# A decoder block on one core: first stage and last sums issued in program order, the norm's scale vector spread by TensorE

## The chip, the cores and the metric

The kernel runs on one core of a Trainium2 chip (trn2). The metric is the device time of one execution in microseconds (us). Three executions of the kernel before took 2191.38, 2193.44 and 2195.94 us; the median, 2193.44 us, is its time here.

The core has five engines that each run their own instructions one after the other: TensorE (PE in the rows, with PEld for its weight loads), VectorE (DVE), ScalarE (ACT), GpSimd (POOL) and SyncE (SP), which here issues most of the DMAs. They wait for each other by semaphores.

## The reference, cut to what matters

One layer, 512 rows of 2048 values in float32:

```python
def rmsnorm(x, g):
    return x * lax.rsqrt(jnp.mean(x * x, axis=-1, keepdims=True) + EPS) * g

h = rmsnorm(x, g_mix_pre)
mix = hybrid_mixer(h, w_in, w_out, ...)      # four attention mixers on the columns of h @ w_in
x = x + rmsnorm(mix, g_mix_post)
h2 = rmsnorm(x, g_mlp_pre)
y = jnp.square(jax.nn.relu(h2 @ w_up)) @ w_down
x = x + rmsnorm(y, g_mlp_post)
```

Only the two ends matter here: the first norm with the few columns of `h @ w_in` that are wanted with rows on the partitions (values of two attention branches, gates and forget logits: 288 columns), and the last norm with its sum.

## The kernel before, in words

Every matrix product is made of three float32r products (high by high, high by low, low by high), so each operand is split: ScalarE casts the high part and VectorE subtracts it to get the low part (`split`, L90 to L92).

**First stage (L160 to L239).** The 512 rows are four tiles `t` of 128 rows. Per tile: a DMA loads `x` (3 buffers); ScalarE squares it with a running sum (L194); GpSimd makes the reciprocal root `r` (L86, L87); VectorE scales four chunks of 512 columns by `r` and by `gB` (L213), the vector `g_mix_pre` on all 128 partitions, loaded by a broadcast DMA of 1 MB (L183); TensorE transposes each chunk in four 128x128 pieces (L154) into one of three PSUM banks `mm`; `split` moves it to `acth` and `actl`. The value weights come in four chunks of 512 rows (L176, 2 buffers `raw`, four DMAs each) and are split to `wvh` and `wvl`. Then 48 matmuls per tile (16 row blocks, three products each; L218 to L220) add up 288 columns in one of two PSUM banks `pt`, and `split` (to `vA`), an exponential (`gates`) and an addition (`fy`) read that bank (L221 to L223). Two small matmuls on a table of the relative bias (L232) and their sums `row` (L233) belong to the stage as well. Behind it come the large projections, `mm<-acth,wh` at L311.

A scheduler at build time puts each engine's instructions in an order of its own, by its estimate of when their inputs are there; it may take matmuls of one tile between those of another, and pieces of later work (such as `wl<-raw,wh`, the split of the first projections' weights) between those of the stage. On the chip an engine then takes its instructions in that order.

**End (L1364 to L1375).** The second product of the MLP ends with a chain of 24 matmuls into bank `a`, 12 for row tile 2 and 12 for row tile 3. For each of the two tiles VectorE adds the bank to `ze` (L1371), ScalarE squares and sums it (L1241), VectorE adds the parts of the sum (L1255) and GpSimd takes the root, VectorE multiplies by `g_mlp_post` (L1246) and adds the scaled result to `x` (L1262, two halves `zn` and `ze`), and DMAs store it (L1264). The `zn` halves of both tiles are squared and scaled shortly before (`done`, L1248; scaled on GpSimd).

Of the kernel before, what the change touches and what calls it, by code (L numbers as in the profile page):

```python
# [10 lines left out]
F32 = mybir.dt.float32  # L11
# [27 lines left out]

@with_exitstack  # L40
def hybrid_block(ctx: ExitStack, tc: tile.TileContext, a, out):
    nc = tc.nc
# [117 lines left out]
    with tc.tile_pool(name="start", bufs=1, reuse_waits="tile") as st:  # L160
# [10 lines left out]
        def load_v(c):  # L171
            raw = wa.r.tile([128, 4, 512], F32, name="raw", tag="raw", bufs=wa.raw)
            ks_ = slice(4 * c, 4 * c + 4)
            o = 0
            for col, w in ((VSA, 128), (VWA, 128), (GA, 24), (FC, 8)):
                nc.sync.dma_start(raw[:, :, o:o + w], w_in_k[:, ks_, col:col + w])  # L176
                o += w
            split(wvh[:, ks_], wvl[:, ks_], raw[:, :, 0:VW])

        gB = st.tile([128, D], F32, name="gB")  # L180
        nc.scalar.dma_start(ident, a["c_ident"])
        load_x(0)
        nc.sync.dma_start(gB, bcast_rows(a["g_mix_pre"], 128, D))  # L183
        load_v(0)
        load_x(1)
        load_x(2)
        load_v(1)
        load_v(2)
        load_v(3)
        ss = st.tile([128, NT], F32, name="ss")  # L190
        junk = st.tile([128, D], mybir.dt.bfloat16, name="junk")
# [5 lines left out]
        rs = [mean_square(0)]  # L197
# [3 lines left out]
        foxb = st.tile([128, 8], F32, name="foxb")  # L201
        nc.scalar.dma_start(foxb, bcast_rows(a["fox_bias"], 128, 8))


        for t in range(NT):
            r = rs[t]
            if t + 1 < NT:
                if t == 0:
                    load_x(3)
                rs.append(mean_square(t + 1))  # L210
            for c in range(4):
                cs = slice(512 * c, 512 * (c + 1))
                nc.vector.scalar_tensor_tensor(xs[t][:, cs], xs[t][:, cs], r[:, 0:1], gB[:, cs],  # L213
                                               op0=OP.mult, op1=OP.mult)
                transpose_into(xs[t][:, cs], t, 4 * c)
            o = bank("pt")
            for k in range(KT):
                nc.tensor.matmul(o[:, 0:VW], acth[:, k, tb(t)], wvh[:, k], start=(k == 0), stop=False)  # L218
                nc.tensor.matmul(o[:, 0:VW], acth[:, k, tb(t)], wvl[:, k], start=False, stop=False)
                nc.tensor.matmul(o[:, 0:VW], actl[:, k, tb(t)], wvh[:, k], start=False, stop=(k == KT - 1))  # L220
            split(vA[:, t, :, 0:64], vA[:, t, :, 64:128], o[:, 0:256].rearrange("p (b d) -> p b d", b=4))  # L221
            nc.scalar.activation(gates[:, t], o[:, 256:280], AF.Exp, scale=-1.0)
            nc.vector.tensor_tensor(y[:, t], o[:, 280:288], foxb, op=OP.add)  # L223
        nc.sync.dma_start(rel, a["rel_bias"])
# [1033 lines left out]
    def final(t, r):  # L1258
        for j in ((0, 1) if t < 2 else (1, 0)):
# [12 lines left out]
    for g, (n, p) in enumerate(rdown.order):  # L1272
# [11 lines left out]
        end = n == END + 1 and p == X  # L1284
        for k, t in ([(k, t) for t in range(2) for k in range(4)] if end else
                     [(k, t) for k in range(4) for t in range(2)]):
            w3(o[:, t], uh[:, k, tb(t)], ul[:, k, tb(t)], wh[:, k], wl[:, k], first and k == 0, k == 3, True)
# [62 lines left out]
        elif p == M7:  # L1350
# [4 lines left out]
            if last:  # L1355
                zop("e", np_, o, OP.add)
                done((2, 3), 1, np_)
        elif p == M3:
# [3 lines left out]
            if last and np_:  # L1362
                for t in range(2):
                    final(t, rstd_last(t))  # L1364
# [4 lines left out]
        else:  # L1369
            for t in (2, 3):  # L1370
# [55 lines left out]
```

## Time and profile before

| | |
|---|---|
| median of three runs | 2193.44 us (2191.38 to 2195.94) |
| the profiled execution's own time | 2192.32 us |
| its span, first to last instruction | 2190.5 us |
| TensorE, VectorE, ScalarE, GpSimd busy | 98%, 78%, 51%, 3% of the span |
| mean granted TensorE clock | 0.995 of full speed |
| first matmul of the large projections | 54.24 us from the span's start |
| last matmul issued, last VectorE instruction done | 2176.37, 2186.36 us |

The rows below come from the profiled execution. Times are from the start of its span. A matmul's duration includes its way through the array, so matmuls of one kind overlap; what a row of them costs is the distance of their starts. Where the table gives a clock of 1.00 TensorE runs at 2.4 GHz, at 0.50 at 1.2 GHz.

### The profile page before, as it was taken

Reading aid. Unit: us, or ns where it says so; the run is one execution under the profiler, and the core shown is the slowest. Engines: PE = TensorE matmul, PEld = TensorE weight load, DVE = VectorE, ACT = ScalarE, POOL = GpSimd, SP = SyncE. Lnnn points to the kernel's source line nnn. Section 1 sums busy time; section 2 is a strip of 40 time slices with the busy share of each in tenths; the row PEclk is TensorE's granted clock in tenths of the full one; section 3 lists DMA queues with packets and bytes.
Section 4 is the critical chain, followed back from the end, with each engine's and each line's share of the span. In section 5 each row is a group of like instructions: output and inputs, shape, how many; then the busy total and the mean of one; then the engine's idle time right before and its main releaser. Section 6 shows DMA issues by size and latency. Waiting matters only on the chain.

```text
span 2190.5 us, 31618 instructions
## 1 busy us (share of the span) xinstructions
PE 2152.4 (98%) x12496; PEld 1891.2 (86%) x12496; DVE 1702.4 (78%) x2405; ACT 1111.6 (51%) x1794; POOL 75.3 (3%) x106
## 2 busy tenths in 40 slices
PE   7999999999999999999999999999999999999997
PEld 6888888887888888889999999999988888888885
DVE  6666667677666442899998898889978888889997
ACT  5446556566666432555665566566553333333343
POOL 1100000000011000100000000000000000000023
PEclk9999999999999999999999999999999999999999
DMA  7443333333333743647556555655874666576453
GB/s 226 137 135 89 99 92 100 88 97 98 100 102 125 250 149 96 199 157 253 186 190 204 199 194 186 216 185 191 303 268 148 231 212 213 170 251 215 163 179 154
DMA packets 371448, 375.26 MB, mean 171 GB/s; under 512 B 17048, under 2 KB 304024, under 8 KB 369508
## 3 DMA queue, kind: packets, MB, share of 16 engines
q1 hardware_dynamic: 370164, 370.36, 51.6%
q8 instruction: 98, 1.61, 0.3%
q0 software_dynamic: 560, 2.03, 0.2%
q10 hardware_dynamic: 576, 0.86, 0.1%
q14 instruction: 50, 0.41, 0.1%
HBM read 298.15 MB, written 77.02 MB: 171 GB/s over the span
## 4 chain that ended last, share of the span: by engine, by line
PE 91%; DVE 6%; ACT 1%; DMA 1%; issue 1%; POOL 1%; SPq 0%; DVEq 0%; POOLq 0%; ACTq 0%
PE mm L311 21%; PE a L812 5%; PE a L811 5%; PE a L813 5%; PE f L811 5%; PE f L812 5%; PE f L813 5%; PE e L811 5%; PE e L812 5%; PE e L813 5%; PE c L813 3%; PE c L811 3%; PE c L812 3%; PE pt L556 2%; PE mm L811 2%; PE mm L813 2%
## 5 line engine op out<-in xcount | busy, mean ns | idle before, releaser
L311 PE MATMUL mm<-acth,wh 128*128 128x512 f32 x704 | 281.8, 400 | 0.0
L311 PE MATMUL mm<-acth,wl 128*128 128x512 f32 x704 | 279.1, 396 | 0.0
L311 PE MATMUL mm<-actl,wh 128*128 128x512 f32 x704 | 278.8, 396 | 0.0
L92 DVE TENSOR_TENSOR wl<-raw,wh 128x512 fp32r<-128x512 f32 x272 | 182.3, 701 | 83.1 <-ACT wh L91 81.5
L91 ACT CAST wh<-raw 128x512 fp32r<-128x512 f32 x272 | 155.6, 618 | 100.9 <-PE mm L813 47.3
L91 ACT CAST sxh<-raw 128x2048 fp32r<-128x2048 f32 x55 | 105.3, 1915 | 187.4 <-DVE raw L1032 92.1
L91 ACT CAST sxh<-place 128x2048 fp32r<-128x2048 f32 (+1 forms) x61 | 111.6, 1829 | 148.7 <-DVE place L1032 42.7
L91 ACT CAST wp<-place 128x1024 fp32r<-128x1024 f32 x121 | 127.2, 1052 | 73.3 <-DVE place L1032 46.4
L92 DVE TENSOR_TENSOR wp<-place,wp 128x1024 fp32r<-128x1024 f32 x121 | 147.5, 1219 | 17.9 <-ACT wp L91 17.9
L311 PEld LDWEIGHTS mm<-acth,wl 128*128 128x128 f32 x704 | 132.4, 188 | 25.2 <-issue 0.2
L92 DVE TENSOR_TENSOR sxl<-raw,sxh 128x2048 fp32r<-128x2048 f32 x55 | 126.8, 2306 | 33.6 <-ACT sxh L91 33.6
L311 PEld LDWEIGHTS mm<-actl,wh 128*128 128x128 f32 x704 | 132.7, 188 | 22.0 <-issue 0.2
L311 PEld LDWEIGHTS mm<-acth,wh 128*128 128x128 f32 x704 | 132.6, 188 | 22.0
L92 DVE TENSOR_TENSOR sxl<-place,sxh 128x2048 fp32r<-128x2048 f32 (+1 forms) x61 | 132.9, 2179 | 13.6 <-ACT sxh L91 13.5
L812 PE MATMUL f<-sxl,wp 128*128 128x256 f32 x480 | 135.8, 283 | 0.0
L811 PE MATMUL f<-sxh,wp 128*128 128x256 f32 x480 | 135.8, 283 | 0.0
L813 PE MATMUL f<-sxh,wp 128*128 128x256 f32 x480 | 135.8, 283 | 0.0
L91 ACT CAST ph<-pt 128x512 fp32r<-128x512 f32 (+4 forms) x168 | 72.5, 432 | 123.0 <-PE pt L556 99.4
L92 DVE TENSOR_TENSOR pl<-pt,ph 128x512 fp32r<-128x512 f32 (+4 forms) x168 | 82.9, 497 | 49.1 <-ACT ph L91 47.1
L91 ACT CAST wp<-raw 128x1024 fp32r<-128x1024 f32 x89 | 93.5, 1053 | 51.5 <-DVE raw L1032 32.5
L92 DVE TENSOR_TENSOR wp<-raw,wp 128x1024 fp32r<-128x1024 f32 x89 | 108.5, 1219 | 12.7 <-ACT wp L91 12.7
L497 ACT ACTIVATE P<-P,nm 128x128 f32<-128x128 f32 (+3 forms) x160 | 88.3, 554 | 45.0 <-DVE nm L495 44.8
(338 smaller groups left out, 6346.9 us busy)
## 6 DMA issues: line engine op xcount, KB each, us to landing
raw<-in_w_in_dram SPq DMA_DIRECT2D x44, 1024.0 KB, 5.3
place<-in_w_down_dram SPq DMA_DIRECT2D x42, 1024.0 KB, 6.8
place<-in_w_up_dram SPq DMA_DIRECT2D x35, 1024.0 KB, 6.8
raw<-in_w_up_dram SPq DMA_DIRECT2D x29, 1024.0 KB, 6.7
u_d<-uh SPq DMA_DIRECT2D x32, 896.0 KB, 3.5
u_d<-uc SPq DMA_DIRECT2D x32, 896.0 KB, 3.5
acth<-u_d SPq DMA_DIRECT2D x56, 512.0 KB, 5.2
actl<-u_d SPq DMA_DIRECT2D x56, 512.0 KB, 5.2
```

What stands on the lines that cost most here:

```text
L91: nc.scalar.copy(h, src)
L92: nc.vector.tensor_tensor(l, src, h.bitcast(F32), op=OP.subtract)
L311: nc.tensor.matmul(o, x[:, k], w[:, k], start=(n == 0), stop=(n == 3 * KT - 1))
L497: nc.scalar.activation(self.views[i], self.views[i], AF.Exp, bias=nm[:, i:i + 1], scale=1.0, accum_out=z[:, i:i + 1])
L556: nc.tensor.transpose(pt[:, tb(i - j)], self.P[:, P_OFF[i] + 128 * j:P_OFF[i] + 128 * (j + 1)], ident)
L811: nc.tensor.matmul(o, xh, wh, start=first, stop=False, skip_group_check=chained)
L812: nc.tensor.matmul(o, xh, wl, start=False, stop=False, skip_group_check=chained)
L813: nc.tensor.matmul(o, xl, wh, start=False, stop=last, skip_group_check=chained)
```

## The change

- A wrapper passes every instruction on and, for the engines in `kept`, tells the scheduler to keep them in program order. All five engines are kept through the first stage, and four (not SyncE) from the last chain on. Instructions of other stages may still be put between kept ones. Since all instructions are now issued in the wrapper, its line (L51) stands for all of them.
- `g_mix_pre` is loaded as four rows of 512 instead of by the broadcast of 1 MB. Eight matmuls with a 0/1 matrix `sel` of 4 rows spread it over the partitions into four PSUM banks, and four VectorE copies bring it to `gB`.
- `x` of the first tile comes in two halves, squared apart. The value weights come in three DMAs per chunk instead of four, two chunks ahead of `x` of the second tile, the others later.
- Program order of the stage: the transposes of a tile stand ahead of the value products of the tile before it; `value_uses` (the readers of bank `pt`) of one tile stand ahead of the scaling of a later tile.
- The last chain's 12 matmuls of row tile 3 go to another bank (`e`), so that tile 2's sum need not wait for them; tile 2's `zn` half is scaled on VectorE; the two tiles' last steps are interleaved.

```diff
 def hybrid_block(ctx: ExitStack, tc: tile.TileContext, a, out):
-    nc = tc.nc
+    nc = InOrder(tc)
...
         def load_x(t):
             xt = st.tile([128, D], F32, name="x", tag="x", bufs=3)
-            nc.sync.dma_start(xt, x2[128 * t:128 * (t + 1)])
+            for c in range(1 if t else 2):
+                cs = slice(0, D) if t else slice(D // 2 * c, D // 2 * (c + 1))
+                nc.sync.dma_start(xt[:, cs], x2[128 * t:128 * (t + 1), cs])
...
-        nc.sync.dma_start(gB, bcast_rows(a["g_mix_pre"], 128, D))
...
+        nc.kept.update(("tensor", "vector", "scalar", "gpsimd", "sync"))
+        nc.scalar.dma_start(sel, a["c_sel"])
+        nc.scalar.dma_start(g4, a["g_mix_pre"].rearrange("o (c n) -> (o c) n", c=4))
...
+            for col, w in ((VSA, 128), (VWA, 152), (FC, 8)):
+                nc.sync.dma_start(raws[c][:, :, o:o + w], w_in_k[:, 4 * c:4 * c + 4, col:col + w])
...
+        def transposed(t, r, between=lambda c: None):
+            scale_x(t, r, 0)
+            for c in range(4):
+                if c < 3:
+                    between(c)
+                    scale_x(t, r, c + 1)
+                transpose_into(xs[t][:, 512 * c:512 * (c + 1)], t, 4 * c)
...
+        spreads = [bank(tag) for tag in ("sc", "sc", "pt", "pt")]
+        for c, gb in enumerate(spreads):
+            nc.tensor.matmul(gb, sel_r[:, tb(c)], gh, start=True, stop=False)
+            nc.tensor.matmul(gb, sel_r[:, tb(c)], gl, start=False, stop=True)
+        def spread_g(c):
+            nc.vector.tensor_copy(gB[:, 512 * c:512 * (c + 1)], spreads[c])
...
+        transposed(0, r, lambda c: spread_g(c + 2) if c < 2 else None)
+        split_v(0)
+        load_v(2)
+        value_products(0, (0,))
+        split_v(1)
+        load_v(3)
+        load_x(2)
+        r = mean_square(1)
+        value_products(0, (1,))
+        transposed(1, r, lambda c: split_v(2) if c == 1 else None)
+        load_x(3)
+        split_v(3)
+        value_products(0, (2, 3))
+        r = mean_square(2)
+        value_uses(0)
+        transposed(2, r)
+        value_products(1, (0, 1, 2, 3))
+        r = mean_square(3)
+        value_uses(1)
+        transposed(3, r)
+        value_products(2, (0, 1, 2, 3))
+        value_uses(2)
+        value_products(3, (0, 1, 2, 3))
+        value_uses(3)
+        nc.kept.clear()
...
+        halves_ = [o[:, t] for t in range(2)]
+        if end:
+            halves_[1] = pd.tile([128, 2, 512], F32, name="e", tag="e")[:, 1]
+            nc.kept.update(("tensor", "vector", "scalar", "gpsimd"))
...
+                    scaled(3, 1, np_, nc.gpsimd)
...
+            last_sum(2)
+            scaled(2, 1, 1, nc.vector)
+            r = rstd_last(2)
+            scaled(2, 0, 1, nc.vector)
+            last_sum(3)
+            final(2, r, (1,))
+            r3 = rstd_last(3)
+            scaled(3, 0, 1, nc.vector)
+            final(2, r, (0,))
+            final(3, r3, (1, 0))
```

The order in which the engines get their instructions moves only in the first stage and at the end; between the two it is the same as before. Three places follow.

TensorE before, where the third tile is transposed (`mm_329` to `mm_353`); `pt_182` and `pt_271` are the value products of the first and second tile, `acth`/`wvh` and so on their operands:

```order
L154 MATMUL mm_329<-ident_71,x_110 128x128 x3
L218 MATMUL pt_182<-wvh_94,acth_85 128x288
L218 MATMUL pt_271<-wvh_94,acth_85 128x288
L154 MATMUL mm_329<-ident_71,x_110 128x128
L154 MATMUL mm_337<-ident_71,x_110 128x128 x4
L154 MATMUL mm_345<-ident_71,x_110 128x128 x4
L232 MATMUL sc_504<-onehot_139,rel_141 24x320
L219 MATMUL pt_182<-wvl_95,acth_85 128x288
```

TensorE now, at the third tile (`x_208`); `pt_189` is the first tile's bank, `pt_328` the second's:

```order
L51 MATMUL pt_189<-wvh_94,actl_86 128x288
L51 MATMUL mm_298<-ident_71,x_208 128x128 x4
L51 MATMUL mm_306<-ident_71,x_208 128x128 x4
L51 MATMUL mm_314<-ident_71,x_208 128x128 x4
L51 MATMUL mm_321<-ident_71,x_208 128x128 x4
L51 MATMUL pt_328<-wvh_94,acth_85 128x288
L51 MATMUL pt_328<-wvl_95,acth_85 128x288
```

Before, the third tile's transposes stood between value products of the first two tiles, 11 of the second tile's 48 being behind `mm_345`; now they stand behind the first tile's last product and ahead of all 48 of the second tile. At the fourth tile it is the same: its 16 transposes stand behind `pt_328` and ahead of the 96 products of the third and fourth.

VectorE now, at the same place (`rs_r_289` is the third tile's root, `wl_563` the split of the first projection's weights):

```order
L51 TENSOR_TENSOR wvl_95<-raw_204,wvh_94 128x1152
L51 TENSOR_TENSOR vA_90<-pt_189,vA_90 128x4x64
L51 TENSOR_TENSOR fy_77<-pt_189,foxb_108 128x8
L51 SCALAR_TENSOR_TENSOR x_208<-x_208,rs_r_289,gB_96 128x512 x2
L51 TENSOR_TENSOR wl_563<-raw_558,wh_562 128x512 x2
L51 TENSOR_TENSOR actl_86<-mm_298,acth_85 128x4x128
L51 SCALAR_TENSOR_TENSOR x_208<-x_208,rs_r_289,gB_96 128x512
L51 TENSOR_TENSOR actl_86<-mm_306,acth_85 128x4x128
L51 SCALAR_TENSOR_TENSOR x_208<-x_208,rs_r_289,gB_96 128x512
L51 TENSOR_TENSOR wl_563<-raw_558,wh_562 128x512
```

Before, VectorE scaled the third tile and three chunks of the fourth ahead of the last chunk of value weights (`wvl<-raw_126`) and ahead of the first `vA`; now the third tile's scaling stands behind `vA` and `fy` of the first tile, and the fourth tile's behind those of the second.

VectorE at the end, now (`a_19217` is tile 2's bank, `e_19218` tile 3's, `place2` and `place1` the two tiles' rows of `x`):

```order
L51 TENSOR_TENSOR ze_15942<-a_19217,ze_15942 128x512
L51 TENSOR_TENSOR zn_15938<-zn_15938,g31_15946 128x512
L51 TENSOR_REDUCE sy_19246<-ssy_15943 128x1
L51 TENSOR_TENSOR ze_15942<-ze_15942,g30_15945 128x512
L51 TENSOR_TENSOR ze_15942<-e_19218,ze_15942 128x512
L51 SCALAR_TENSOR_TENSOR place2_9107<-zn_15938,rs_r_19248,place2_9107 128x1024
L51 TENSOR_REDUCE sy_19256<-ssy_15943 128x1
L51 TENSOR_TENSOR ze_15942<-ze_15942,g30_15945 128x512
L51 SCALAR_TENSOR_TENSOR place2_9107<-ze_15942,rs_r_19248,place2_9107 128x1024
L51 SCALAR_TENSOR_TENSOR place1_9106<-zn_15938,rs_r_19258,place1_9106 128x1024
```

Before, the two additions from bank `a` stood together ahead of everything else here, and each tile's sum of squares, gain and final additions followed as one piece; now tile 2's sum of squares and gain stand ahead of tile 3's addition, and tile 3's sum of squares and gain stand between tile 2's two final additions.

## Rows read from the trace of the kernel before

**Rows 1.** The page: busy time, share of the span and instructions.

```profile
PE 2152.4 (98%) x12496; PEld 1891.2 (86%) x12496; DVE 1702.4 (78%) x2405; ACT 1111.6 (51%) x1794; POOL 75.3 (3%) x106
```

**Rows 2.** Busy time by stretch; columns in the first line.

```profile
core 0: us, PE busy (x) PEld busy (x) DVE busy (x) ACT busy (x) POOL busy (x), PEclk, DMA share, GB/s
...
10.00:16.40 6.40, 5.25 (x28) 4.64 (x28) 6.07 (x9) 3.94 (x6) 0.00 (x0) 1.00 1.03 354
16.40:19.40 3.00, 0.00 (x0) 0.02 (x1) 0.84 (x2) 2.52 (x3) 0.79 (x2) 1.00 0.90 216
19.40:27.00 7.60, 6.89 (x31) 6.34 (x32) 7.15 (x10) 6.05 (x9) 1.49 (x2) 0.55 0.76 228
27.00:54.20 27.20, 27.20 (x203) 25.78 (x203) 18.56 (x33) 11.89 (x25) 2.17 (x4) 1.00 0.70 189
54.20:70.00 15.80, 15.80 (x72) 13.06 (x71) 8.85 (x26) 4.78 (x11) 3.33 (x6) 1.00 0.40 143
```

**Rows 3.** TensorE in 0:54.2 us, by line: count, busy us, mean ns.

```profile
L232 PE MATMUL sc<-onehot,rel 32*24 32x320 f32 x4 | 1.4, 436 | 0.0
```

**Rows 4.** Timeline of TensorE: start us, us, engine, line, operation.

```profile
15.39 0.30 PE L218 MATMUL pt<-wvh,acth 128*128 128x288 f32 x1
15.52 0.29 PE L219 MATMUL pt<-wvl,acth 128*128 128x288 f32 x1
...
47.62 0.66 PE L154 MATMUL mm<-ident,x 128*128 128x128 f32 x4
...
54.24 0.40 PE L311 MATMUL mm<-acth,wh 128*128 128x512 f32 x1
```

**Rows 5.** Timeline of VectorE in the first stage.

```profile
9.58 2.74 DVE L213 SCALAR_TENSOR_TENSOR x<-x,rs_r,gB 128x512 f32<-128x512 f32 x4 [9.58 <-DMA gB<-in_g_mix_pre_dram]
...
13.21 1.36 DVE L92 TENSOR_TENSOR wvl<-raw,wvh 128x1152 fp32r<-128x1152 f32 x1 [0.29 <-ACT wvh L91]
14.48 1.88 DVE L92 TENSOR_TENSOR actl<-mm,acth 128x512 fp32r<-128x512 f32 x3
...
40.34 4.89 DVE L92 TENSOR_TENSOR wl<-raw,wh 128x512 fp32r<-128x512 f32 x8
...
48.38 0.47 DVE L233 TENSOR_TENSOR row<-sc,cadd 24x320 f32<-24x320 f32 x1
...
66.56 0.68 DVE L710 COPY kk<-mm 64x511 f32<-64x511 f32 x1
```

**Rows 6.** Timeline of ScalarE and VectorE behind the last value product.

```profile
54.44 0.37 ACT L91 CAST vA<-pt 128x256 fp32r<-128x256 f32 x1 [5.53 <-PE pt L220]
...
55.52 0.17 DVE L223 TENSOR_TENSOR fy<-pt,foxb 128x8 f32<-128x8 f32 x1 [0.26 <-ACT gates L222]
```

**Rows 7.** Timeline of SyncE's queue and of ScalarE: the last chunk of value weights.

```profile
24.98 2.02 SPq L176 DMA_DIRECT2D raw<-in_w_in_dram  x4
...
29.76 1.16 ACT L91 CAST wvh<-raw 128x1152 fp32r<-128x1152 f32 x1 [1.92 <-DMA raw<-in_w_in_dram]
```

**Rows 8.** DMA issues of the first 60 us: count, size, median us to landing.

```profile
raw<-in_w_in_dram SPq DMA_DIRECT2D x3, 1024.0 KB, 7.7
...
bias_rep<-bias_row POOLq DMA_DIRECT2D x1, 1920.0 KB, 10.3
```

**Rows 9.** Timeline of VectorE at the end.

```profile
2173.38 1.21 DVE L1268 TENSOR_TENSOR ze<-ze,f 128x1024 f32<-128x1024 f32 x1
2176.80 1.29 DVE L1371 TENSOR_TENSOR ze<-a,ze 128x512 f32<-128x512 f32 x2 [2.21 <-PE a L813]
...
2179.84 1.28 DVE L1262 SCALAR_TENSOR_TENSOR place<-zn,rs_r,place 128x1024 f32<-128x1024 f32 x1 [0.75 <-POOL rs_r L87]
...
2183.75 1.28 DVE L1262 SCALAR_TENSOR_TENSOR place<-zn,rs_r,place 128x1024 f32<-128x1024 f32 x1 [0.76 <-POOL rs_r L87]
2184.95 1.41 DVE L1262 SCALAR_TENSOR_TENSOR place<-ze,rs_r,place 128x512 f32<-128x512 f32 x2
```

**Rows 10.** Timeline of GpSimd at the end.

```profile
2175.74 2.52 POOL L1246 TENSOR_TENSOR zn<-zn,g 128x512 f32<-128x512 f32 x2
```

More of the change, by code (lines that the diff above doesn't have):

```diff
@@ L201, in hybrid_block @@
         foxb = st.tile([128, 8], F32, name="foxb")
+        nc.kept.update(("tensor", "vector", "scalar", "gpsimd", "sync"))
+        nc.scalar.dma_start(sel, a["c_sel"])
+        nc.scalar.dma_start(g4, a["g_mix_pre"].rearrange("o (c n) -> (o c) n", c=4))
+        nc.scalar.dma_start(ident, a["c_ident"])
         nc.scalar.dma_start(foxb, bcast_rows(a["fox_bias"], 128, 8))
[L205 to L210, printed above, removed]
-            for c in range(4):
[L212 to L217, printed above, removed]
+        raws = {}
@@ L218, in hybrid_block, with value_products @@
+        values = {}
+        def value_products(t, chunks):
+            if t not in values:
+                values[t] = bank("pt")
+            o = values[t]
+            for k in range(4 * chunks[0], 4 * chunks[-1] + 4):
                 nc.tensor.matmul(o[:, 0:VW], acth[:, k, tb(t)], wvh[:, k], start=(k == 0), stop=False)
@@ L223, in hybrid_block @@
             nc.vector.tensor_tensor(y[:, t], o[:, 280:288], foxb, op=OP.add)
+        load_x(0)
+        load_v(0)
+        load_v(1)
+        load_x(1)
+        nc.vector.tensor_copy(sel_r, sel)
+        split(gh, gl, g4)
+        spreads = [bank(tag) for tag in ("sc", "sc", "pt", "pt")]
[4 more added lines that the diff above has]
+            nc.vector.tensor_copy(gB[:, 512 * c:512 * (c + 1)], spreads[c])
+        for c in range(2):
+            cs = slice(D // 2 * c, D // 2 * (c + 1))
+            nc.scalar.activation(junk[:, cs], xs[0][:, cs], AF.Square, scale=D ** -0.5, accum_out=ss2[:, c:c + 1])
+        nc.gpsimd.tensor_tensor(ss[:, 0:1], ss2[:, 0:1], ss2[:, 1:2], op=OP.add)
+        r = rstd_of(st, ss[:, 0:1])
+        spread_g(0)
+        spread_g(1)
+        transposed(0, r, lambda c: spread_g(c + 2) if c < 2 else None)
[23 more added lines that the diff above has]
+        nc.kept.clear()
         nc.sync.dma_start(rel, a["rel_bias"])
@@ L1256, in rstd_last, with final @@
         return rstd_of(dp, s1)
-    def final(t, r):
-        for j in ((0, 1) if t < 2 else (1, 0)):
+    def final(t, r, columns):
+        for j in columns:
             for m in (range(2) if (t, j) == (NT - 1, 0) else (slice(0, 2),)):
@@ L1356, in hybrid_block @@
                 zop("e", np_, o, OP.add)
-                done((2, 3), 1, np_)
+                if np_:
+                    squares(2, 1, np_)
+                    squares(3, 1, np_)
+                    scaled(3, 1, np_, nc.gpsimd)
+                else:
+                    done((2, 3), 1, np_)
         elif p == M3:
@@ L1369, in hybrid_block, with last_sum @@
         else:
-            for t in (2, 3):
-                nc.vector.tensor_tensor(z["e"][:, 1, t % 2], o[:, t % 2], z["e"][:, 1, t % 2], op=OP.add)
+            def last_sum(t):
+                nc.vector.tensor_tensor(z["e"][:, 1, t % 2], halves_[t % 2], z["e"][:, 1, t % 2], op=OP.add)
                 squares(t, 0, 1)
-                r = rstd_last(t)
-                scaled(t, 0, 1, nc.vector)
-                final(t, r)
+            last_sum(2)
[8 more added lines that the diff above has]
+            final(3, r3, (1, 0))
     pd_.__exit__(None, None, None)
```

62 lines of the change are left out of this document (40 added, 22 removed).

## The prediction

> **What bounds the kernel now.** I read the page first, then the stretches of the two ends, then the engines' timelines there. The page has TensorE busy for 98% of the span [rows 1]; the table of stretches says where it was not. It works for 5.25 us from 10 to 16.4 us, not at all from 16.4 to 19.4, and from 19.4 to 27 us at a mean granted clock of 0.55; from 27.0 to 54.2 us it is busy for 27.20 of 27.20 us at full clock, and just so from 54.2 to 70 us in the large projections [rows 2]. So the first stage ends as TensorE's work: the first projection's matmul starts at 54.24 us [rows 4], and what comes later there is, with TensorE as full behind it, later at the end. The scheduler had mixed the value products of several tiles, so that one of them could always go. The other open place is the end: after the last sums VectorE, ScalarE and GpSimd work in a chain until 2184.95 + 1.41 = 2186.36 us [rows 9], with the stores and the end of the span 4.1 us behind.
>
> The span is 2190.5 us, the execution 2192.32 us; that is 1.1 us under the median of 2193.44 us. I add to 2192.3.
>
> **The first stage, part by part.** I follow the new order with durations of before. The prices: a value product costs 0.133 us (starts 15.39 and 15.52), a tile's 48 of them 6.4 us; four transposes cost 0.5 us, being 0.66 with the last one's way through [rows 4]; the `row` matmuls 1.4 us in all [rows 3]. On VectorE, back to back, a scaled chunk is 2.74/4 = 0.69 us, a low part of an activation chunk 1.88/3 = 0.63 us, of a weight piece 4.89/8 = 0.61 us, of a chunk of value weights 1.36 us, a `row` 0.47 us, a copy out of PSUM 0.68 us [rows 5].
>
> *Scale vector.* The broadcast of 1 MB goes; VectorE's first scaling had waited for it until 9.58 us [rows 5], and now waits for the root. The eight spreading matmuls lie in time when TensorE is idle anyway. But two of the four copies stand between the first tile's scalings: 1.4 us. Against that the low part of the first value weights (1.36 us), which stood between, now comes after. I keep the end of the first tile's activations where it was, 14.48 + 1.88 = 16.4 us. Bounds: 15 to 17.5, by the four copies (2.7 us) more or the 1.36 us less.
>
> *Up to the first tile's last product.* On VectorE then follow, in order, a `row`, two chunks of value weights, a `row`: the first chunk ends at 18.2, the second tile's scaling starts at 20.1 us. The buffer of the third chunk is free only at 18.2, and SyncE issues its load then. From such an issue to the cast that waited for it were 29.76 - 24.98 = 4.8 us [rows 7]: 23.0 us, cast 1.16, low part 1.36: 25.5 us. VectorE waits there in its own order; behind stand two scalings and three activation chunks, 3.3 us, then the fourth chunk, 1.36: 30.2 us. TensorE's last 12 products of the first tile follow, 1.6 us: 31.8 us. Of the 15.4 us since 16.4 it has worked some 10: 6.4 of products, 2 of transposes, 1.4 of `row` matmuls.
>
> *First wait.* The third tile's 16 transposes stand ahead of all 48 products of the second tile, whose operands are long ready. The third tile's scaling stands on VectorE behind `vA` and `fy` of the first, which need its last product. From ScalarE's copy at 54.44, right behind a last product, to the end of `fy` at 55.69 took 1.3 us [rows 6]: 33.1 us. Then VectorE has four scalings and, by the order shown, two weight pieces and two activation chunks among them: 4 x 0.69 + 2 x 0.61 + 2 x 0.63 = 5.2 us, and the last four transposes 0.5 us: 38.8 us. TensorE waits for 7.0 us with 2 us of work in it. Before, it had those products to do. Now the second tile's 48 end at 45.2 us.
>
> *Second wait.* The same at the fourth tile: 1.3 us, four scalings and two activation chunks 4.0 us, some 0.5 us for the first transposes and their cast, 0.5 us for the last: 51.5 us. The remaining 96 products have nothing to wait for: 12.8 us, 64.3 us, against 54.24. That is **+10.1 us** at full clock.
>
> *Clock.* Before, after the idle 3.0 us, the granted clock was 0.55 over 7.6 us [rows 2], so some 6.8 us of them at 0.50 (1.2 GHz), in which up to 3.4 us were lost; 54.24 has that in it. Now there are three stretches with little TensorE work (17 to 30, 32 to 39, 45 to 51 us), and behind each a block of products that sets the end. If each is followed by what followed the one before, up to 3.4 us each are lost: 0 to 10 us. The stretches are not empty, as that one was; I take 2.5 us, nearer to none.
>
> *Loads.* The `row` sums are done at 20 us instead of 49 [rows 5], and with them `bias_rep`, 1.9 MB in 10.3 us [rows 8], moves from behind the stage into it, beside the third and fourth tile of `x` and the first two projections' weights, which took 7.7 us each when less was beside them [rows 8]; the DMA engines had a share of 0.70 from 27 us on as it was [rows 2]. Pieces of those weights stand among the third tile's instructions on VectorE and ScalarE, so a late load holds up the transposes. Nothing to 3 us; I take 1.0 us. The Trainium skill says that DMAs issued from SyncE, ScalarE and GpSimd run on the same 16 engines and interleave ("DMA: Bandwidth & Descriptors", rules for kernel authors); by it GpSimd's queue gives `bias_rep` no way past the weights, and the term would be nearer to 3 us than to none. No row here has the two side by side.
>
> Sum of the stage: 10.1 + 2.5 + 1.0 = **+13.6 us**, the first projection at 67.8 us; the bounds give +9 to +24.
>
> **The end.** Tile 2's products are done 12 matmuls earlier, but VectorE is busy with `ze` until 2173.38 + 1.21 = 2174.6 us, so tile 2's sum starts then and not at 2176.80 [rows 9]. From there: four operations of the sum's size (1.29/2 = 0.65 us: the sum, the `zn` gain, the `ze` gain, tile 3's sum) and some 0.5 us of squares, reduction and handing over: 2177.7 us. GpSimd has one `zn` gain less, 2.52/2 = 1.26 us, and is free at 2177.0; from its last gain's end, 2178.26, to the first final addition, 2179.84, were 1.6 us [rows 9, 10]: the addition now starts at 2178.6. From there to the end were 2186.36 - 2179.84 = 6.5 us, with 0.76 us of waiting for the second root [rows 9]; that wait goes, since a final addition of tile 2 covers it. 2178.6 + 5.8 = 2184.4: **-2.0 us**, between -1.0 (the stores come closer together, and bank `a` gives less than I think) and -2.6.
>
> The middle has the same order on every engine: 0. Together 2192.3 + 13.6 - 2.0 = **2203.9 us**, 0.48% above the median.
>
> **The rivals.**
>
> 1. *Half clock behind every wait, and late weights.* 64.3 + 8.5 + 3 = 75.8 us to the first projection: 2192.3 + 21.6 - 2.0 = 2212 us. For it: one idle stretch before was enough. Against it: from 10 to 16.4 us TensorE had pauses too, and the clock shown is 1.00 [rows 2]. The Trainium skill tells of a kernel in which every wait between short groups of matmuls lets the next one start at the low clock ("TensorE: Matmul & The Clock Gate", HAM oscillation); by that this rival would be the likelier one. The trace has one case that agrees, and none with some work in the pause.
> 2. *The stage gains.* If the third and fourth tiles are scaled in time, TensorE has from 16.4 us on only its work: 25.6 of products, 6 of transposes, 1.4 of `row` matmuls, 33.0 us, and the first projection starts at 49.4 us: 2192.3 - 4.8 - 2.0 = 2185.5 us. For it: the 1 MB load is gone and the second chunk of weights comes early. Against it: the readers of a bank stand ahead of the next scaling on VectorE in the order itself, so each tile's transposes start behind the last product of another. It decides only if the two waits together fall under 3 us.
> 3. *The later stages take the delay up.* If what follows is set by VectorE or by loads, the stage's loss vanishes and the end's gain stays: 2190.3 us. For it: VectorE is busy for 78% of the span [rows 1]. Against it: TensorE is full from 54.2 to 70 us, and VectorE has 8.85 of 15.80 us there [rows 2].
>
> **How the numbers follow.** Forecast 0.68, its own range 2198 to 2208; rival 1, 0.14; rival 2, 0.08; rival 3, 0.07; the rest, 0.03, lies between. What a measurement of this kernel can tell from no change is about 0.2%, 4.4 us: slower is above 2197.8, faster below 2189.1. Slower: the forecast and rival 1, 0.82. Same: rival 3 and most of the rest, 0.09. Faster: rival 2 and a little of the rest, 0.09. The range, 2196 to 2210, takes in the forecast and what lies between it and its neighbours on both sides.
>
> **What would show it.** In the profile after, the first 128x512 matmul on `acth` and `wh` starts at 64 to 70 us; TensorE has two pauses of 6 to 8 us with 16 transposes in each, ended by VectorE's scaling; VectorE idles ahead of `wvl` of the third chunk, for a DMA; the copies to `gB` take 0.6 to 0.7 us each; the granted clock is 0.50 in a stretch behind at least one pause. At the end the last VectorE instruction ends 8 us behind the last matmul's start instead of 10. I am wrong if the third tile's transposes run before the first tile's last product, or if the first projection starts before 58 us.

## The result, and the profile after

The changed kernel takes 2208.87 us (median of 4 runs, 2207.04 to 2210.22), the kernel before 2192.41 us (2191.19 to 2195.94): a ratio of 1.0074, interval 1.0062 to 1.0086. The profiled execution took 2209.5 us, its span is 2207.7 us: 17.2 us more than before. Slower was forecast, by 11.6 us; the time lies in the range, 5 us above the forecast.

Matched instruction by instruction, TensorE's timeline now lies 21.36 us behind that of before at the first projection (54.24 before [rows 4], 75.60 now), 21.33 us at 900 us, and 18.49 us from 1000 us to the last matmul; the last VectorE instructions end 17.1 us apart. So the stage costs **+21.4 us**, one place near 957 us gives back **-2.9 us**, and the end gives **-1.4 us**. I had +13.6, 0 and -2.0.

First the page of the changed kernel; it answers to [rows 1], and tells nothing: a share over the whole span hides all three places. (All its lines are one helper's, so its groups are told apart by their tiles.)

```profile
PE 2165.5 (98%) x12504; PEld 1898.3 (86%) x12504; DVE 1709.4 (77%) x2412; ACT 1112.1 (50%) x1797; POOL 75.2 (3%) x106
```

The stage from its first transposes to the first projection, by the table of stretches (columns as in [rows 2]); first the kernel before, then the changed one.

```profile
9.70:54.24 44.54, 39.38 (x261) 36.82 (x261) 32.92 (x52) 24.40 (x40) 4.49 (x8) 0.92 0.77 222
```

```profile
9.70:75.60 65.90, 49.00 (x260) 42.47 (x261) 34.61 (x54) 24.92 (x40) 4.68 (x8) 0.84 0.53 167
...
46.50:54.00 7.50, 7.39 (x51) 7.16 (x49) 4.19 (x7) 3.38 (x6) 1.49 (x2) 0.89 0.73 214
54.00:60.70 6.70, 3.03 (x16) 2.27 (x17) 4.76 (x9) 2.25 (x5) 0.00 (x0) 0.82 0.22 77
60.70:66.00 5.30, 5.30 (x26) 5.30 (x26) 1.18 (x2) 0.59 (x1) 0.00 (x0) 0.58 0.37 39
66.00:75.60 9.60, 9.60 (x74) 9.60 (x73) 0.59 (x2) 0.56 (x2) 0.00 (x0) 1.00 0.01 2
```

TensorE's idle time goes from 5.2 to 16.9 us, and its busy time from 39.4 to 49.0 us for nearly the same number of instructions (261 and 260): so 11.7 us are waits and 9.6 us are the same work done more slowly. From 60.7 to 66 us 26 matmuls run at a granted clock of 0.58 (mostly the level of 1.2 GHz), then 74 in 9.6 us at 2.4 GHz. TensorE's timeline of the changed kernel shows the waits:

```profile
18.16 0.61 PE L51 MATMUL pt<-wvh,acth 128*128 128x288 f32 x1
...
24.53 1.03 PE L51 MATMUL mm<-ident,x 128*128 128x128 f32 x8
...
29.00 1.08 PE L51 MATMUL mm<-ident,x 128*128 128x128 f32 x4 [3.44 <-DVE x L51]
...
38.23 1.34 PE L51 MATMUL mm<-ident,x 128*128 128x128 f32 x8 [2.05 <-issue]
44.59 1.09 PE L51 MATMUL mm<-ident,x 128*128 128x128 f32 x4 [5.02 <-DVE x L51]
...
46.58 0.59 PE L51 MATMUL pt<-wvh,acth 128*128 128x288 f32 x1
...
55.98 1.33 PE L51 MATMUL mm<-ident,x 128*128 128x128 f32 x8 [2.08 <-issue]
58.76 1.09 PE L51 MATMUL mm<-ident,x 128*128 128x128 f32 x4 [1.45 <-DVE x L51]
...
60.76 0.59 PE L51 MATMUL pt<-wvh,acth 128*128 128x288 f32 x1
...
75.60 0.40 PE L51 MATMUL mm<-acth,wh 128*128 128x512 f32 x1
```

The third tile's transposes stand behind the first tile's last product and ahead of the second tile's first (46.58), the fourth's ahead of the third's (60.76), as forecast. What ends the first of these waits is read on ScalarE, with the issue of the load on SyncE's queue and VectorE's rows behind it:

```profile
25.17 0.58 ACT L51 CAST acth<-mm 128x512 fp32r<-128x512 f32 x1 [4.56 <-PE mm L51]
...
36.22 0.37 ACT L51 CAST vA<-pt 128x256 fp32r<-128x256 f32 x1 [1.29 <-PE pt L51]
37.08 0.19 ACT L51 ACTIVATE gates<-pt 128x24 f32<-128x24 f32 x1 [0.49 <-DVE vA L51]
41.24 1.14 ACT L51 CAST wh<-raw 128x512 fp32r<-128x512 f32 x2 [3.97 <-DMA raw<-in_w_in_dram]
...
53.93 0.37 ACT L51 CAST vA<-pt 128x256 fp32r<-128x256 f32 x1 [3.96 <-PE pt L51]
```

```profile
28.22 0.38 SPq L51 DMA_DIRECT2D raw<-in_w_in_dram  x1
```

```profile
25.78 0.69 DVE L51 TENSOR_TENSOR actl<-mm,acth 128x512 fp32r<-128x512 f32 x1 [2.77 <-ACT acth L51]
26.84 1.36 DVE L51 TENSOR_TENSOR wvl<-raw,wvh 128x1152 fp32r<-128x1152 f32 x1 [0.36 <-ACT wvh L51]
...
41.89 1.29 DVE L51 TENSOR_TENSOR wl<-raw,wh 128x512 fp32r<-128x512 f32 x2 [3.10 <-ACT wh L51]
```

Two pieces of the first projection's weights stand ahead of the third tile's activations, and their DMA, issued at 28.22 us, is there only at 41.24: 13.0 us, where these loads took 7.7 us before [rows 8]. `bias_rep` was issued at 26.56 us and took 12.3 us, so it moved beside this load until some 38.9 us; two tiles of `x`, issued from 22.36 us on, stood ahead of the load in SyncE's queue. VectorE, which needs these pieces, idles 3.10 us for them. The DMA table from 34 to 38 us (packets, MB, share of the 16 DMA engines) shows the queue that carries `bias_rep` (q0) with most of the engines and SyncE's (q1) with little:

```profile
q0 software_dynamic: 210, 1.03, 61.7%
q1 hardware_dynamic: 474, 0.24, 21.2%
```

The place near 957 us, first before, then after, on TensorE's timeline:

```profile
954.06 0.39 PE L813 MATMUL mm<-acth,wl 128*128 128x512 f32 x1
957.96 0.39 PE L811 MATMUL a<-acth,wp 128*128 128x256 f32 x1 [3.51 <-ACT v L1111]
```

```profile
975.07 0.39 PE L51 MATMUL mm<-acth,wl 128*128 128x512 f32 x1
975.30 0.28 PE L51 MATMUL a<-acth,wp 128*128 128x256 f32 x1
```

The engines have the same order there in both kernels; a wait of 3.5 us is gone, and some 1.1 us of what that gave is lost again in the next 50 us. And VectorE's end, which answers to [rows 9]; the last matmul starts at 2194.86:

```profile
2193.18 0.69 DVE L51 TENSOR_TENSOR ze<-a,ze 128x512 f32<-128x512 f32 x1
2193.79 1.04 DVE L51 TENSOR_TENSOR zn<-zn,g 128x512 f32<-128x512 f32 x1
...
2194.82 1.69 DVE L51 TENSOR_TENSOR ze<-ze,g 128x512 f32<-128x512 f32 x1
...
2197.26 1.28 DVE L51 SCALAR_TENSOR_TENSOR place<-zn,rs_r,place 128x1024 f32<-128x1024 f32 x1
...
2200.87 1.28 DVE L51 SCALAR_TENSOR_TENSOR place<-zn,rs_r,place 128x1024 f32<-128x1024 f32 x1 [0.46 <-POOL rs_r L51]
2202.07 1.41 DVE L51 SCALAR_TENSOR_TENSOR place<-ze,rs_r,place 128x512 f32<-128x512 f32 x2
```

From the last matmul's start to VectorE's end were 9.99 us and are 8.62.

### The profile page after: what moved, and what is told of

Read it like the earlier page. It is cut to its first block, busy times and chain, and to the rows that moved or that the text cites. A ratio compares the mean times of both kernels' runs of the same rounds, so it can differ in the third digit from the quotient of the medians.

```text
span 2207.7 us, 31642 instructions
## 1 busy us (share of the span) xinstructions
PE 2165.5 (98%) x12504; PEld 1898.3 (86%) x12504; DVE 1709.4 (77%) x2412; ACT 1112.1 (50%) x1797; POOL 75.2 (3%) x106
## 4 chain that ended last, share of the span: by engine, by line
PE 89%; DVE 7%; ACT 1%; issue 1%; DMA 1%; POOL 1%; POOLq 0%; DVEq 0%; SPq 0%; ACTq 0%
PE mm L51 26%; PE f L51 15%; PE a L51 15%; PE e L51 15%; PE c L51 7%; PE sc L51 5%; PE pt L51 4%; PE ov L51 2%; DVE sxl L51 1%; DVE raw L51 1%; DVE s L51 1%; DMA raw<-in_w_in_dram 1%; DVE wl L51 1%; DVE place L51 0%; DVE actl L51 0%
## 5 line engine op out<-in xcount | busy, mean ns | idle before, releaser
L51 PE MATMUL mm<-acth,wh 128*128 128x512 f32 (+1 forms) x768 | 303.4, 395 | 0.0
L51 PE MATMUL mm<-acth,wl 128*128 128x512 f32 (+1 forms) x768 | 300.6, 391 | 0.0
L51 PE MATMUL mm<-actl,wh 128*128 128x512 f32 (+1 forms) x768 | 300.3, 391 | 0.0
L51 DVE TENSOR_TENSOR wl<-raw,wh 128x512 fp32r<-128x512 f32 x272 | 182.8, 702 | 86.4 <-ACT wh L51 84.7
L51 ACT CAST wh<-raw 128x512 fp32r<-128x512 f32 x272 | 155.9, 618 | 104.9 <-PE mm L51 77.9
L51 ACT CAST sxh<-raw 128x2048 fp32r<-128x2048 f32 x55 | 105.3, 1915 | 188.1 <-DVE raw L51 92.5
L51 ACT CAST sxh<-place 128x2048 fp32r<-128x2048 f32 (+1 forms) x61 | 111.6, 1829 | 148.0 <-DVE place L51 46.3
L51 PE MATMUL f<-sxh,wp 128*128 128x256 f32 x960 | 182.9, 283 | 0.9 <-DVE wp L51 0.9
L51 PEld LDWEIGHTS mm<-acth,wl 128*128 128x128 f32 x768 | 144.5, 188 | 26.4 <-issue 0.2
L51 PEld LDWEIGHTS mm<-actl,wh 128*128 128x128 f32 x768 | 144.8, 189 | 23.2 <-issue 0.2
L51 PEld LDWEIGHTS mm<-acth,wh 128*128 128x128 f32 x768 | 144.7, 188 | 23.3
L51 ACT CAST wp<-place 128x1024 fp32r<-128x1024 f32 x121 | 127.0, 1051 | 73.4 <-DVE place L51 46.6
L51 DVE TENSOR_TENSOR wp<-place,wp 128x1024 fp32r<-128x1024 f32 x121 | 147.7, 1221 | 17.9 <-ACT wp L51 17.9
L51 PEld LDWEIGHTS f<-sxh,wp 128*128 128x128 f32 x960 | 154.0, 192 | 1.4 <-DVE wp L51 1.1
L51 DVE TENSOR_TENSOR sxl<-raw,sxh 128x2048 fp32r<-128x2048 f32 x55 | 126.9, 2308 | 33.5 <-ACT sxh L51 33.5
L51 DVE TENSOR_TENSOR sxl<-place,sxh 128x2048 fp32r<-128x2048 f32 (+1 forms) x61 | 133.1, 2183 | 13.6 <-ACT sxh L51 13.5
L51 PE MATMUL f<-sxl,wp 128*128 128x256 f32 x480 | 135.8, 283 | 0.0
L51 ACT CAST ph<-pt 128x512 fp32r<-128x512 f32 (+4 forms) x168 | 72.5, 432 | 123.0 <-PE pt L51 120.5
L51 DVE TENSOR_TENSOR pl<-pt,ph 128x512 fp32r<-128x512 f32 (+4 forms) x168 | 83.0, 497 | 49.0 <-ACT ph L51 47.1
L51 ACT CAST wp<-raw 128x1024 fp32r<-128x1024 f32 x89 | 93.4, 1051 | 50.1 <-DVE raw L51 32.5
L51 DVE TENSOR_TENSOR wp<-raw,wp 128x1024 fp32r<-128x1024 f32 x89 | 108.5, 1221 | 11.2 <-ACT wp L51 11.2
L51 ACT ACTIVATE P<-P,nm 128x128 f32<-128x128 f32 (+3 forms) x160 | 88.3, 555 | 44.9 <-DVE nm L51 44.8
```

What stands on the lines that cost most here:

```text
L51: ins = f(*args, **kw)
```

## The experiments

In this table "first projection" is the start of its first matmul in the profiled execution; the ratio is to the kernel before, run on the same chip. The experiments ran on three chips, on which the medians of the kernel before were 2192.30 to 2193.13 us; where two rows lie close together, I compare both their medians and their ratios.

| kernel | median, us (lowest to highest, runs) | ratio, 95% interval | first projection |
|---|---|---|---|
| before | 2192.41 (2191.19 to 2195.94, 4) | 1 | 54.24 |
| changed | 2208.87 (2207.04 to 2210.22, 4) | 1.0074, 1.0062 to 1.0086 | 75.60 |
| 1 end only | 2191.13 (2189.37 to 2193.40, 11) | 0.9993, 0.9984 to 1.0002 | 54.13 |
| 2 banks only | 2192.03 (2191.07 to 2194.37, 11) | 1.0000, 0.9991 to 1.0009 | 53.16 |
| 3 stage not held | 2187.17 (2186.62 to 2188.12, 11) | 0.9977, 0.9968 to 0.9986 | 52.80 |
| 4 bias late | 2206.67 (2205.26 to 2208.88, 5) | 1.0066, 1.0054 to 1.0079 | 71.62 |
| 5 waits filled | 2209.81 (2209.77 to 2212.66, 5) | 1.0081, 1.0069 to 1.0094 | 73.11 |
| 6 early scaling | 2200.67 (2200.46 to 2202.75, 5) | 1.0039, 1.0026 to 1.0052 | 67.58 |
| 7 both 4 and 6 | 2201.93 (2201.30 to 2202.23, 5) | 1.0041, 1.0028 to 1.0055 | 67.56 |
| 8 as 3, banks as before | 2189.22 (2188.05 to 2191.38, 11) | 0.9987, 0.9978 to 0.9996 | 52.94 |
| 9 as 3, end as before | 2189.00 (2188.10 to 2191.14, 11) | 0.9982, 0.9974 to 0.9991 | 52.05 |
| 10 as 5, start filled too | 2210.73 (2210.41 to 2212.04, 5) | 1.0081, 1.0067 to 1.0095 | 73.98 |

**1. The end alone.** The kernel before with the diff's parts from `final` on.

> The kernel before with only the change of the end. The theory of the three places (first stage +21.4 us, start of the second up-projection -2.9, end -1.4, as the two traces stand to each other): only the end moves, the last VectorE instruction ends 8.6 us behind the last matmul's start instead of 10.0, the time is 1 to 2 us below the kernel before (2190.4 to 2191.4). What I had predicted for this part was -2.0. Rival: the -2.9 us at the start of the second up-projection also come from this edit; then the time is 4.2 us below, near 2188.

2191.13 us, 1.8 us under the median of the kernel before on that chip (2192.91 us), though the interval takes in 1. In the profile the last VectorE instruction ends 8.61 us behind the last matmul's start, as expected, and the wait near 957 us is still 3.5 us. It speaks for the three places and against the rival.

**2. The banks alone.**

```diff
+        for tag in ("sc", "sc", "pt", "pt"):
+            bank(tag)
         rs = [mean_square(0)]
```

> The kernel before, in which only the PSUM banks are laid out in another order: the pool's tags sc and pt are asked for ahead of mm, as the spreading of the scale vector does it. No instruction is added or moved. Theory: TensorE's wait of 3.5 us ahead of the first 128x256 matmul on a and wp (at 957.96 us) is a wait for the bank, which ScalarE still reads as an mm bank; with another layout the matmul starts at some 954.3 us, and the time is 2.5 to 3.5 us below the kernel before (2189 to 2190). Rival: that wait depends on how far the other engines are ahead, or on the loads; then the matmul still waits 3.5 us and the time is the same as before within 0.5 us.

TensorE's timeline at the place, with no wait:

```profile
953.12 0.39 PE L815 MATMUL mm<-acth,wl 128*128 128x512 f32 x1
953.35 0.28 PE L813 MATMUL a<-acth,wp 128*128 128x256 f32 x1
```

So the wait was for the bank: the layout of the banks alone takes it away. But the median moved by 0.9 us only, and the ratio is 1.0000: the expected 2.5 to 3.5 us did not come. In the profile TensorE, 1.0 us ahead of the kernel before until 950 us, is 4.6 us ahead at 958 us and 2.0 us from 1000 us on: of the 3.6 us it gave 2.6 back, mostly in waits for VectorE's `wp` (2.8 us from 950 to 1000 us). At the end it lost another 1.6 us, where it ran at a granted clock of 0.72 behind a wait for `sxl`. What the layout is worth is left to the eighth run. The first projection starts 1.08 us earlier here though no instruction of the stage was touched: two profiles of the same stage can lie that far apart.

**3. The stage not held.** The changed kernel without the two lines that hold it:

```diff
-        nc.kept.update(("tensor", "vector", "scalar", "gpsimd", "sync"))
...
-        nc.kept.clear()
```

> The changed kernel, but the first stage is not held in program order: the scheduler places its instructions; the scale vector through TensorE, the halved first load and the joined weight loads stay. Theory that the order is what costs: the first projection starts at 50 to 57 us instead of 75.60, and with the gains of the other two places the time is 2184 to 2191 us. Rival, that the scale vector's copies, the weights' loads or the half clock at the start cost: the first projection starts above 62 us and the time stays above 2196.

2187.17 us, 21.7 us under the changed kernel (21.3 by the ratios): the order in which the stage is held costs all of its loss. The order of all five engines was set free at once, that of SyncE's loads with it. With the spread scale vector and the joined loads the scheduler does the stage in 1.4 us less than before, which is little more than the 1.08 us of the second run. TensorE's row for the stage shows 3.7 us of idle time and the busy time of the kernel before:

```profile
9.70:52.80 43.10, 39.44 (x263) 36.17 (x261) 34.49 (x55) 24.02 (x42) 4.68 (x6) 1.00 0.68 203
```

This version is faster than both kernels, by more than the interval.

**4. The bias rows behind the stage.** `nc.kept.clear()` moved behind the two `bias` stores, so that `rel` to `bias_rep` too keep the program's order.

> The changed kernel with the row sums and the loads and stores around them (rel, onehot, bias_row, bias_rep) held behind the last value product, so that bias_rep's 1.9 MB no longer move beside the first projection's weights. Theory that the loads term was mis-sized: these weights land near 36 us instead of 41, ScalarE's and VectorE's pieces of them no longer hold up the third tile's transposes, the first wait falls from 10.4 to about 7 us and the time by 3 to 4 us, near 2205. Rival: the weights are late for other loads' sake or the wait is VectorE's own; then the wait stays near 10 us, and the time moves by under 1.5 us.

The first wait, from ScalarE's copy of `vA` (35.83) to the second tile's first product (42.63), is 6.8 us, where it was 10.4. ScalarE's timeline has no wait for the weights any more:

```profile
35.83 0.37 ACT L51 CAST vA<-pt 128x256 fp32r<-128x256 f32 x1 [1.44 <-PE pt L51]
...
41.35 0.58 ACT L51 CAST acth<-mm 128x512 fp32r<-128x512 f32 x1 [1.54 <-PE mm L51]
41.83 1.14 ACT L51 CAST wh<-raw 128x512 fp32r<-128x512 f32 x2
```

The first projection starts 4.0 us earlier; the median is 2.2 us lower, where 3 to 4 were expected. The first wait lost 3.6 us, and what is left is near the 7.0 us I had worked out for it. But the edit did two things: the load no longer ran beside `bias_rep`, and the scheduler put the two pieces of weights behind the third tile's scalings, where they had stood among them. The part of the late load alone is VectorE's idle time of 3.10 us in the changed kernel; the rest was not taken apart.

**5. The waits filled.** Products that nobody reads, into a bank of tag `ov`:

```diff
+                for _ in range(((0,) * 4, (0, 0, 16, 0), (12,) * 4, (10,) * 4)[t][c]):
+                    nc.tensor.matmul(filler[:, 0:VW], acth[:, 0, tb(0)], wvh[:, 0], start=True, stop=True)
                 transpose_into(xs[t][:, 512 * c:512 * (c + 1)], t, 4 * c)
```

> The changed kernel with 104 more products of 128x288 into a bank that nobody reads, on operands long ready, placed on TensorE ahead of the transposes of the second (16), third (48) and fourth tile (40), that is in its three waits. Theory of the clock: the products behind the waits then run at 0.13 us each instead of 0.24 for their first part, the second tile's from 7.3 to 6.4 us, the last two tiles' from 15.0 to some 13, the first tile's last 24 from 5.2 to some 3.2; the waits themselves stay, and the first projection starts 3 to 5 us earlier, at 70.5 to 72.5 us, the time near 2205. Rival: the clock costs little, since the waits are set by VectorE and a DMA; then the first projection stays within 1.5 us of 75.6, or comes later by what the added products push.

TensorE's timeline behind the filled first wait: the products are 0.13 us apart almost at once.

```profile
45.52 0.60 PE L51 MATMUL mm<-ident,x 128*128 128x128 f32 x4
45.88 0.38 PE L51 MATMUL pt<-wvh,acth 128*128 128x288 f32 x1
46.09 0.29 PE L51 MATMUL pt<-wvl,acth 128*128 128x288 f32 x1
46.22 0.29 PE L51 MATMUL pt<-wvh,actl 128*128 128x288 f32 x1
```

The second tile's products take 6.7 us instead of 7.35 (45.88 to ScalarE's copy at 52.54), the last two tiles' 12.9 instead of 14.8 (60.24 to 73.11). The second wait grew from 6.8 to 7.7 us, since the added products were in its way. The first projection came 2.5 us earlier, a little under what was expected. The time did not follow: against the changed kernel 0.7 us was lost ahead of 970 us, 1.8 us near 1010 us, mostly in a wait of 1.3 us for `wp`, and 1.6 us at a granted clock of 0.71 and 0.79 at the end. The loss near 1010 us is there in the tenth run too (a wait of 1.5 us, 2.1 us in all) and in none of runs 4, 6 and 7: it comes with the added products or their bank, and which of the two was not tested. For the stage this run shows the clock's share; as a way to a faster kernel it is nothing.

**6. The scaling earlier.**

```diff
         r = mean_square(2)
-        value_uses(0)
+        r3 = mean_square(3)
         transposed(2, r)
+        value_uses(0)
         value_products(1, (0, 1, 2, 3))
-        r = mean_square(3)
+        transposed(3, r3)
         value_uses(1)
-        transposed(3, r)
```

> The changed kernel with another program order for the same work: the third tile's scaling stands ahead of the first tile's vA and fy on VectorE, the fourth tile's ahead of the second's, and the fourth tile's mean square ahead of the first tile's copy on ScalarE. TensorE's order is the same. Theory that the place of a bank's readers ahead of the next scaling makes the two waits: the third tile's transposes end near 38 us instead of 46.6, and the second wait falls from 6.9 to 3 to 5 us, since pieces of the late weights still stand in it; the first projection starts at 62 to 67 us, the time is 8 to 13 us below the changed kernel's. Rival: the late loads alone make both waits, then under 4 us is gained.

8.2 us under the changed kernel, at the lower end of what was expected; the first projection, at 67.58 us, just misses its 62 to 67. The place of the bank's readers ahead of the next scaling, with the earlier mean square that goes with it, is a good third of the 21.7 us. The third tile's transposes end at 41 us, not 38, since VectorE waits for that tile's root until 35.09. The pieces of the late weights still stood among the fourth tile's scalings.

**7. Both.**

> Both edits, the early scaling and the bias rows held behind the stage. Theory that waits and loads are all that is left beside TensorE's own work: the first projection starts at 57 to 62 us, the time is 2190 to 2195 us. Rival, that holding an order loses what mixing tiles gained, whatever the order: it stays above 64 us.

The expected 57 to 62 us did not come; the rival's sign, above 64 us, did. The first projection starts at 67.56 us as without the later bias rows. On VectorE the scheduler, which still places what isn't held, had put seven weight pieces among the fourth tile's scalings:

```profile
43.55 1.41 DVE L51 SCALAR_TENSOR_TENSOR x<-x,rs_r,gB 128x512 f32<-128x512 f32 x2
44.88 4.29 DVE L51 TENSOR_TENSOR wl<-raw,wh 128x512 fp32r<-128x512 f32 x7
50.28 0.69 DVE L51 TENSOR_TENSOR actl<-mm,acth 128x512 fp32r<-128x512 f32 x1 [1.10 <-ACT acth L51]
50.89 0.74 DVE L51 SCALAR_TENSOR_TENSOR x<-x,rs_r,gB 128x512 f32<-128x512 f32 x1
```

The gains of 4 and 6 do not add up. That every held order loses is not shown by two of them: which instruction's place makes up the 14.8 us between this order and the mixed one was not taken apart.

**8. The unheld stage with the banks as before.**

```diff
-        spreads = [bank(tag) for tag in ("sc", "sc", "pt", "pt")]
+        spreads = [bank(tag) for tag in ("mm", "mm", "mm", "pt")]
```

> The kernel with the unheld first stage (the third experiment), in which the four spread rows lie in three mm banks and one pt bank, so that the PSUM banks have the layout of the kernel before. Theory: TensorE again waits 3.5 us ahead of the first matmul on a and wp, and the time goes from 2187.2 to 2189 to 2190. Rival: the layout's gain is given back behind it in waits for VectorE's wp; then the wait is there, but the time stays within 1 us of 2187.2.

The wait is back, on the same instruction:

```profile
953.21 0.39 PE L51 MATMUL mm<-acth,wl 128*128 128x512 f32 x1
957.13 0.39 PE L51 MATMUL a<-acth,wp 128*128 128x256 f32 x1 [3.54 <-ACT v L51]
```

2189.22 against 2187.17 us, 11 runs each, whose ranges hardly touch: the layout is worth 2.05 us in this kernel, 2.2 us by the ratios. In the kernel before, by the second run, it was worth nothing that the times show.

**9. The unheld stage with the end as before.**

> The kernel with the unheld first stage (the third experiment) and the end of the kernel before. Theory: the end is worth the 1.3 us by which the last VectorE instruction stands closer behind the last matmul in the two traces; the time goes from 2187.2 to 2188.2 to 2188.8. What I had predicted for the end, 2.0 us, would give 2189.2. Rival: the end gives nothing, since another wait there takes its place: 2187.2.

2189.00 against 2187.17 us: the end is worth 1.83 us by the medians, 1.1 us by the ratios; the first run had 1.8 and 1.5 us. In the profile the last VectorE instruction ends 9.99 us behind the last matmul's start, as in the kernel before. These times cannot tell the 2.0 us I had predicted from the 1.4 us by which the distance differs in the traces.

**10. The start filled too.**

```diff
+                for _ in range((0, 0, 6, 2)[c] if t == 0 else 0):
+                    nc.tensor.transpose(filler[:, 0:128], xs[0][:, 0:128], ident)
```

> The fifth experiment's kernel with 8 more transposes of the first tile's first chunk into the unread bank, 6 ahead of the third and 2 ahead of the fourth group of the first tile's transposes, to close two pauses of 1.4 and 0.2 us there. Theory of the clock, that pauses among the first tile's transposes keep the following products at 0.24 us: these run at 0.13 us from some 18.2 us on, not from 24.0, the second tile's transposes come 2 us earlier and the first projection starts at 70 to 72 us instead of 73.11. Rival: the first products are slow for another reason (so early, whatever stands ahead); then they stay at 0.24 us until 24 us, and the first projection stays at 73 us or comes later.

The expected 70 to 72 us did not come, and the run is inconclusive. The first products did run 0.13 us apart from 18.4 us on, but from 19.7 us on 0.24 us apart, behind two pauses of 0.54 and 0.99 us. The first tile was done 2.1 us earlier than in the changed kernel (ScalarE's copy at 34.13, not 36.22; in the fifth run it was at 35.58), and ScalarE then waited 4.24 us for the weights, until 39.43: the gain went into the wait for the load. The first projection, at 73.98 us, is no earlier than in the fifth run.

## Why the prediction came out as it did

- *Direction and mechanism of the stage: right.* The two waits are there, each with 16 transposes in it, behind one tile's last product and ahead of the next tile's first; the first is longer than the 6 to 8 us named. Copies to `gB` took 0.68 us. The third run shows that the held order is the cause, the sixth that the place of `vA` and `fy` ahead of the next scaling is a good part of it.
- *Its size: 13.6 forecast, 21.4 measured.* By the chain of the forecast, with its numbers first: first tile's last product 31.8, 36.2; first wait 7.0, 10.4; second tile's products 6.4, 7.35; second wait 6.3, 6.8; last two tiles 12.8, 14.8. The differences, 4.4 + 3.4 + 0.95 + 0.5 + 2.0, make the 11.3 us from 64.3 to 75.6, for which I had put 2.5 us of clock and 1.0 us of loads.
- *The loads were mis-sized:* 1.0 forecast; 3.1 us of VectorE's idle time in the first wait, and 3.6 us less of that wait in the fourth run, which also moved the two pieces. I had bounded them by 3 and taken 1. The Trainium skill's rule that the queues share 16 engines ("DMA: Bandwidth & Descriptors", rules for kernel authors) pointed to the upper end, and the trace agrees: from 34 to 38 us q0, with `bias_rep`, had 61.7% of the engines and SyncE's queue, with the weights, 21.2%.
- *The clock was mis-sized:* 2.5 forecast. Behind the two waits alone it is 3.0 us (0.95 + 2.0), which the fifth run took back but for 0.3 us. Of the first tile's 4.4 us the tenth run took back 2.1; whether the rest is clock stays open. I had argued that these stretches were not empty and so would cost less than the empty one of before. By the size of each that held, 0.95 and 2.0 us against up to 3.4; but 16 transposes in a wait did not keep the block behind it at 2.4 GHz, and near to none was wrong. The Trainium skill ("TensorE: Matmul & The Clock Gate", HAM oscillation) tells of waits between groups of matmuls that each let the next start at the low clock. Both blocks behind the waits agree (0.24 us between their first products).
- *One step was wrong in kind.* I had VectorE wait for the third chunk's DMA. It waited for TensorE, through ScalarE's cast at 25.17: the second tile's transposes stood until 24.53 behind 24 products, most of them at half clock. And the second tile's scaling came at 21.6 instead of 20.1, since its mean square stood on ScalarE behind two casts of weights. So the third chunk's low part was done at 28.20 us, not 25.5 (VectorE's rows above): 2.7 of the first tile's 4.4 us. Three more waits of VectorE for ScalarE's casts (0.62, 0.57 and 0.36 us) are 1.5 us of the rest.
- *The middle was wrong:* 0 forecast, -2.9 in the profiles, some -2.1 by the times of runs 3 and 8, and nothing by those of the second run. I had reasoned from the order of instructions, which is the same. What moved is where tiles lie: the spread rows ask for `sc` banks first, so the pool's layout changes. That the layout makes the wait is shown, by its going in the second run and its return in the eighth; that a bank which the next pool takes over is free earlier is how I read it. The wait of 3.5 us stood in the trace of before.
- *The end was right, if a little large:* 2.0 forecast, 1.4 in the profiles (9.99 to 8.62 us, and the same in runs 9 and 1), 1.1 to 1.8 by the times. What is short of it: two gains on VectorE took 1.04 and 1.69 us beside GpSimd's, not 0.65, and a wait of 0.46 us for the second root was left.
- *The rivals.* The first, half clock behind every wait and late weights, gave 75.8 us for the first projection, and 75.60 came: in kind it was right for the stage. That its number fits so well is luck in part: it put 8.5 us on the clock, and shown are 3.0 us behind the two waits and 2.1 us in the first tile. Its total of 2212 us was too high by the bank's gain. Against it I had held that TensorE paused from 10 to 16.4 us too and the clock shown was 1.00. That column misled me, as the last section says: in the trace of before the first tile's 16 transposes took 3.15 us, from 10.38 to the first product at 13.53, where my price for them was 2.0, so TensorE was slow there as well. With this read rightly, rival 1 deserved more than 0.14. Rival 2 fell, since the scaling was not in time. Rival 3 fell, since TensorE carried 21.3 us of delay unchanged to 900 us. That the forecast total was only 5 us off is luck in part: the stage was 7.8 us too small, and the middle, with 2.9 us that I did not have, took some of that back.

## What to carry to other kernels

TensorE had independent work for its waits here, and the order written out by hand that forbade the mixing paid three times: for the wait, for the slow clock of the block behind it, and for loads that now landed inside it. Where the program leaves such work, check an order by hand against these three. When a price is bounded from both sides and each stretch has its own pause, price each block behind a pause by the slow stretch that the trace does show, as an upper bound, and do not put the sum near nothing. And before the unchanged part is put at zero, look for waits on buffers there: allocating tiles in another order can move them with no instruction moved.

## What the runs showed of the hardware

The granted clock's column can read full speed while matmuls run slowly, so that 1.00 does not always mean 2.4 GHz. This stretch of the changed kernel has 1.00, and its products start 0.24 us apart until 24.06 us and 0.13 us apart behind:

```profile
18.00:24.50 6.50, 6.17 (x25) 5.69 (x25) 4.11 (x5) 2.60 (x3) 1.55 (x3) 1.00 0.64 169
```

The trace of before has such a stretch too, inside 10 to 16.4 us, where the column shows 1.00 [rows 2]:

```profile
10.38 3.39 PE L154 MATMUL mm<-ident,x 128*128 128x128 f32 x16 [10.38 <-DVE x L213]
13.53 0.38 PE L218 MATMUL pt<-wvh,acth 128*128 128x288 f32 x1
```

Early in a trace the spacing of equal matmuls is the safer reading. Between the first products it fell to 0.13 us at 14.9 us before, at 24.1 us in the changed kernel, at 20.3 us in the third run.

The same wait is not always followed by the same clock. TensorE waits 2.1 us for `sxl` near the end in every one of these kernels; in the profiles of runs 2, 5, 6 and 8 some 1.6 us were then lost at a lower granted clock (0.72 in two stretches of the second run), in the others none.
